# A hybrid decoder layer on one core: attention heads held two and four groups into an ordered stretch, and a longer trail in the output projection's last part

## The chip, the cores and the metric

One core of one Trainium2 chip. The metric is the device time of one launch in microseconds, median of the runs shown; lower is better. Times inside an execution (spans, windows, durations) come from one profiled execution.

## What is computed

One decoder layer on 256 tokens of width 2048, in float32, cut from the reference:

```python
x = layer_norm(alpha * x + 0.5 * swiglu(x, ffn1_w_gate, ffn1_w_up, ffn1_w_down), ln1_g, ln1_b)
p = x @ w_in                                        # columns of both mixers
o_attn = diff_attn_group(p[..., :3072], ...)        # 8 heads, ALiBi, causal, p1 - lam * p2
o_rwkv = rwkv7_group(p[..., 3072:], ...)            # 16 heads of size 64, delta rule over the sequence
mix = concatenate([o_attn, o_rwkv], -1) @ w_out     # (256, 2048) @ (2048, 2048)
x = layer_norm(alpha * x + mix, ln2_g, ln2_b)
x = layer_norm(alpha * x + 0.5 * swiglu(x, ffn2_w_gate, ffn2_w_up, ffn2_w_down), ln3_g, ln3_b)
```

The change lies in the product with `w_out`, in what runs beside it (the last attention heads and the end of the RWKV part), and in its passage to LN2 and the second feed-forward.

## The kernel before

**Products.** All dense products go through one `Stream`. A float32 operand is cut into a high part (`wh`, ScalarE, L142) and the remainder (`wl`, VectorE, L145), and each product becomes three matmuls per 128 rows of K: high by high (L152), high by `wl` (L153), low by high (L154). Activations are cut in the same way by `split` into `xh` (L89) and `xl` (L90). The weights stream in once. A *pair* is two K tiles of 128 rows by 512 columns of weights (512 KB, loaded by SyncE's queue into one of three `raw` buffers). The 256 tokens are two halves, `tt` 0 and 1; a pair is used by each half in turn, six matmuls a half (a *product half*). The loop `block` cuts a pair, runs its first half at once, and puts it on `pend`; the second half runs once more than `lag` pairs are pending. In the stage "mix" there are `nw` = 5 cut buffers, used in turn, and `lag` = 2; the sums of a block of 512 columns go to one of three accumulator banks `acc0` to `acc2`, also in turn, when the block's first product half is issued.

**Background work.** Everything else of the mixers is written as Python generators. After every pair `run_bg` lets them issue a step. Outside the ordered stretch a credit decides how much; in it (`even` is true) each generator issues one step per pair (a step that yields 0 runs on into the next), in the order in which they were started.

**Order on the engines.** Each instruction's engine is fixed by the code; the order of an engine's instructions is made at build time by a planner, which goes by the order of writing as a priority and by its own estimate of when an instruction is ready. All engines then run in order. In two of the output projection's three parts the order on TensorE is not the planner's: `manual_schedule` keeps that part's TensorE instructions in the order of writing. What was written before that stretch is still placed by the planner.

**The output projection.** `W_out` has 16 K tiles: four each of the attention groups 0 and 1 and of the RWKV groups 0 and 1. `parts = [(0, 2), (1,), (3,)]`, so part one multiplies attention group 0 and RWKV group 0 (16 pairs: 4 blocks of 512 columns by 4), part two attention group 1 (8 pairs), part three RWKV group 1 (8 pairs). Before each part `ready` runs to the end the generators that make its operand and cuts the operand by `split`. Parts one and two are the ordered stretch. The pairs of part one are counted here from 0 to 15.

**What runs beside it.** At the start of part one three generators are open. One is the RWKV group 1 chain: it loads its 32 by 32 inverses through ScalarE's DMA queue (`TT<-dY`, L845; `YT`, L849), transposes B and K (L807, copies L809), combines (L858, L869), and runs four chunks (L886, L894, L902, L919, L925). The other two are attention group 1, two heads each: heads 4 and 6, and heads 5 and 7. A head passes these steps, one per pair:

- scores: eight matmuls (L1023) into two banks of tag `at`, read by VectorE (L1025)
- maxima (L1028), exponentials on ScalarE (L1033), scaling and difference (L1035 to L1039)
- transposes (L1044) into a bank `at`, copied to `pT` (L1046; one buffer)
- value product (L1053 to L1055) into a bank `at`, squares of it on ScalarE (L1063, L1066)
- norm: a power on POOL (L1070), VectorE's small steps, and a scaling that reads the bank (L1077)
- transposes back (L1081) into a bank `at`, copied by VectorE into `q` (L1082)

There are two banks `at`. Both generators have passed the transposes of their first head when part one begins, so that both issue the value product after pair 0, the norm after pair 1, and so on; the second heads' scores fall after pair 3.

**The end.** In part three `o_done` adds each finished block to `y` (L326), takes statistics (L328), and after the fourth block `ln_tail` normalises (L341, L349), transposes (L83) and cuts the result as the operand of the second feed-forward. That stage's first block uses seven cut buffers, of which the first five are the same as in the mix stage, beginning again at buffer 0; the last pair of part three holds that buffer. TensorE's order in part three is the planner's.

Of the kernel before, what the change touches and what calls it, by code (L numbers as in the profile page):

```python
# [31 lines left out]
NW = {"ffn": 7, "mix": 5}  # L32
# [7 lines left out]
def build(tc, A, out):  # L40
# [58 lines left out]
    class Stream:  # L99
        def __init__(self):  # L100
            self.pend = []
            self.tail = []
            self.roles = None
            self.behind = []
            self.acc = {}
            self.bg = []
            self.credit = {}
            self.hooks = {}
            self.step = 0
            self.slot = 0  # L110
            self.even = False

        def phase(self, name, pool, banks=None):
            assert not self.pend
            self.name, self.pool, self.banks, self.slot, self.rot = name, pool, banks, 0, 0
            self.buffers(NW[name], LAG[name])
# [170 lines left out]
        def run_bg(self):  # L287
            if self.even:
                for g in list(self.bg):
                    while g in self.bg:  # L290
                        try:
                            if next(g) != 0:
                                break
                        except StopIteration:
                            self.bg.remove(g)
                return
            for g in list(self.bg):
                c = self.credit[g]
                c[0] = min(c[0], 0.0) + c[1]
                while c[0] > 0 and g in self.bg:  # L300
                    try:
                        cost = next(g)
                    except StopIteration:
                        self.bg.remove(g)
                        break
                    if cost is None:
                        break
                    c[0] -= cost
# [13 lines left out]
    stream = Stream()  # L322
# [232 lines left out]
    def mix(mp, pq, C):  # L555
# [87 lines left out]
        def rwkv_start(g, prev=None):  # L643
            gr = Group(g)
            st = {"prev": prev, "group": gr}
            if prev is not None:
                prev["next"] = st
            st["gen"] = rwkv_group(g, st)
            stream.spawn(st["gen"], BG)
            return st  # L650
# [342 lines left out]
        def attn_cols(g):  # L993
            st = {"q": qq[:, g],
                  "k": hp.tile([P, 4, S], F32, tag=HT["k"], name=nm("k"))}

            def qkdone(tt, acc, n):
                chan_major(acc, tt, [P] * 4, lambda tr: SC.copy(out=st[n][:, :, tt * P:(tt + 1) * P], in_=tr))
                if n == "q" and tt == 1:
                    st["left"] = 2  # L1000
                    st["gens"] = [attn_heads(g, st, (i, i + 2)) for i in range(2)]
                    for x in st["gens"]:
                        stream.spawn(x, AT)

            stream.block(w_in, AW + g * NB, NB, KX, x_lhs, lambda tt, acc: qkdone(tt, acc, "k"))
            stream.block(w_in, g * NB, NB, KX, x_lhs, lambda tt, acc: qkdone(tt, acc, "q"))
            return st
# [80 lines left out]
        def gens(*sts):  # L1088
            return [g for st in sts for g in [st.get("gen"), st.get("gen2")] + st.get("gens", []) if g is not None]

        r1 = rwkv_start(0)
        rwkv_cols(0, r1, (1, 0, 2))
        r2 = rwkv_start(1, r1)
        a1 = attn_cols(0)
# [4 lines left out]
        a2 = attn_cols(1)  # L1099
# [7 lines left out]
        def ready(q):  # L1107
            stream.drain(gens((a1, a2, r1, r2)[q]))
            for tt in range(2):
                split(res[q][:, :, tt * P:(tt + 1) * P], oT, tt, q)  # L1110
# [16 lines left out]
        def o_done(tt, acc, n, i):  # L1127
            c = slice(n * NB, (n + 1) * NB)
            if i == 0:
                rc = mp.tile([P, NB], F32, tag="tm", name=nm("rc"), bufs=2)  # L1130
                nc.scalar.dma_start(out=rc, in_=xs[tt][:, c])
                V.scalar_tensor_tensor(out=y[tt][n], in0=rc, scalar=ALPHA, in1=acc, op0=ALU.mult, op1=ALU.add)
            elif i < len(parts) - 1:
                V.tensor_tensor(out=y[tt][n], in0=y[tt][n], in1=acc, op=ALU.add)
            else:
                ln_stats(tt, y[tt][n], acc, st[tt], n)
                if n == 3:
                    ln_tail(tt, y[tt], st[tt], gb[0], gb[1], False)
# [3 lines left out]
        def part(i, qs):  # L1142
            if i == 0:
                yt = [hp.tile([P, 4, NB], F32, tag="J0", name=nm("y")), mp.tile([P, 4, NB], F32, tag="BKc", name=nm("y"))]
                y.extend([yt[n // 2][:, 2 * (n % 2) + t, :] for n in range(4)] for t in range(2))
            if 3 in qs:
                gb.extend(load_gb(mp, A["ln2_g"], A["ln2_b"], "J1", "Q"))
            ks = [(4 * q + j, 4 * q + j) for q in qs for j in range(4)]
            for n in range(4):
                stream.block(A["w_out"][0], n * NB, NB, ks, o_lhs, lambda tt, acc, n=n, i=i: o_done(tt, acc, n, i))  # L1150

        for i, qs in enumerate(parts):
            for q in qs:
                ready(q)
                import os
                if os.environ.get("DBG"): print("DBG", i, q, [(k, x.gi_frame and x.gi_frame.f_lineno) for k, st_ in (("a1",a1),("a2",a2),("r1",r1),("r2",r2)) for x in gens(st_)])
            stream.even = i < len(parts) - 1
            with tc.manual_schedule(engines={mybir.EngineType.PE}) if stream.even else ExitStack():
                part(i, qs)

# [34 lines left out]
    with tc.tile_pool(name="mp", bufs=1) as mp, tc.tile_pool(name="pq", bufs=1, space=bass.MemoryType.PSUM) as pq:  # L1195
        stream.phase("mix", mp)
        mix(mp, pq, C)
        stream.flush()
# [43 lines left out]
```

## Time and profile before

| what | value |
|---|---|
| time, median of 3 runs | 1924.98 us (1924.58 to 1926.66) |
| profiled execution's own time | 1924.33 us |
| its span | 1922.5 us, mean granted TensorE clock 0.992 |
| TensorE busy | 1886.7 us, 98% of the span |
| VectorE, ScalarE, POOL busy | 85%, 57%, 4% |
| HBM traffic | 198 GB/s over the span |
| parts one and two of the output projection | about 1072 to 1183 us |
| part three | about 1183 to 1208 us |

How to read the lines below. A line of the timeline gives start and length in us, engine, line of the kernel, operation, what is written from what, and how many instructions were merged; in brackets stands the idle time of the engine before it and who ended it. A line of waits gives engine, line and releaser, then the total us, the times, and the longest. A line of windows gives the window, its length, and for each engine busy us and instructions, then the granted clock of TensorE (1.00 is full), the share of the DMA engines' time and GB/s. Matmuls overlap, so their rate is read from the distance of their starts. `ACTq` is an instruction that ScalarE's queue spends on a DMA.

### The profile page before, as it was taken

The page shows a single profiled execution, that of the slowest core. Times are in us where ns is not written, and L with a number is a line of the kernel's source. Part 1 is how long each engine was busy: PE and PEld are TensorE (multiplying, and loading weights), DVE is VectorE, ACT ScalarE, POOL GpSimd, SP SyncE. Part 2 cuts the span into 40 slices and gives each one's busy share as a digit, 9 for nine tenths or more (in the row PEclk, how much of TensorE's full clock was granted, in tenths as well). Part 3 has the DMA queues.
Part 4 walks back from the last instruction along what each step waited for, and adds up shares of the span by engine and source line. Part 5 has one row for each costly group of instructions (what it writes and reads, how often), then busy time and mean ns, then how long its engine had stood idle before and what let it go on. Part 6 is the DMA issues. An engine that isn't in the chain of part 4 may idle for free.

```text
span 1922.5 us, 24938 instructions
## 1 busy us (share of the span) xinstructions
PE 1886.7 (98%) x9335; PEld 1551.1 (81%) x9335; DVE 1625.3 (85%) x1834; ACT 1094.3 (57%) x1376; POOL 72.5 (4%) x110
## 2 busy tenths in 40 slices
PE   9999999999999999999999899999999999999997
PEld 7788888888888878887878678788888888888886
DVE  7999987789999976777678767999999778999996
ACT  5656665466666536656555544566666545666651
POOL 0000101100000000000000000000000110000000
PEclk9999999999999999999999899999999999999999
DMA  8756676666667456555445445775566676566744
GB/s 307 250 195 221 186 238 224 223 217 202 218 212 226 139 185 195 169 153 154 143 118 160 135 149 193 245 260 195 192 217 222 210 247 216 197 204 211 232 151 133
DMA packets 207320, 381.72 MB, mean 199 GB/s; under 512 B 23530, under 2 KB 25648, under 8 KB 206944
## 3 DMA queue, kind: packets, MB, share of 16 engines
q1 hardware_dynamic: 182928, 350.53, 55.1%
q0 software_dynamic: 6832, 15.32, 3.0%
q10 hardware_dynamic: 17440, 14.29, 2.5%
q8 instruction: 73, 1.20, 0.2%
q14 instruction: 47, 0.39, 0.1%
HBM read 368.29 MB, written 11.80 MB: 198 GB/s over the span
## 4 chain that ended last, share of the span: by engine, by line
PE 59%; DVE 3%; ACT 1%; issue 1%; DMA 0%; ACTq 0%; DVEq 0%
PE acc L152 18%; PE acc L153 17%; PE acc L154 17%; DVE wl L145 1%; DVE y L341 1%; PE sm L785 1%; DVE y L349 0%; PE tr L580 0%; PE tr L439 0%; PE at L1023 0%; PE pr L727 0%; ACT wh L142 0%; DVE xl L90 0%; PE sm L886 0%; DMA dY<-Y 0%
## 5 line engine op out<-in xcount | busy, mean ns | idle before, releaser
L142 ACT CAST wh<-raw 128x1024 fp32r<-128x1024 f32 (+2 forms) x833 | 852.6, 1047 | 616.2 <-PE acc L154 397.4
L145 DVE TENSOR_TENSOR wl<-raw,wh 128x1024 fp32r<-128x1024 f32 (+2 forms) x833 | 984.0, 1214 | 206.2 <-ACT wh L142 202.0
L153 PE MATMUL acc<-wl,xh 128*128 128x512 f32 (+1 forms) x1552 | 605.7, 392 | 1.1 <-DVE wl L145 1.1
L154 PE MATMUL acc<-wh,xl 128*128 128x512 f32 (+1 forms) x1552 | 604.2, 391 | 0.5 <-DVE xl L90 0.5
L152 PE MATMUL acc<-wh,xh 128*128 128x512 f32 (+1 forms) x1552 | 600.1, 394 | 2.3 <-ACT xh L89 2.3
L152 PEld LDWEIGHTS acc<-wh,xh 128*128 128x128 f32 x1552 | 292.5, 189 | 64.1 <-ACT xh L89 3.8
L154 PEld LDWEIGHTS acc<-wh,xl 128*128 128x128 f32 x1552 | 292.6, 189 | 61.0 <-DVE xl L90 0.9
L153 PEld LDWEIGHTS acc<-wl,xh 128*128 128x128 f32 x1552 | 292.5, 189 | 60.2 <-DVE wl L145 1.7
L223 DVE TENSOR_TENSOR raw<-raw,raw 128x2048 f32<-128x2048 f32 x112 | 256.0, 2286 | 1.6 <-DMA raw<-in_ffn_w_up_dram 0.6
L153 PE MATMUL acc<-wl,hh 128*128 128x512 f32 x544 | 212.0, 390 | 0.0
L154 PE MATMUL acc<-wh,hh 128*128 128x512 f32 x544 | 211.4, 389 | 0.0
L152 PE MATMUL acc<-wh,hh 128*128 128x512 f32 x544 | 210.9, 390 | 0.0
L152 PE MATMUL acc<-wh,s 128*128 128x512 f32 x448 | 175.1, 391 | 1.8 <-ACT acc L249 1.0
L154 PE MATMUL acc<-wh,s 128*128 128x512 f32 x448 | 174.6, 390 | 0.0
L153 PE MATMUL acc<-wl,s 128*128 128x512 f32 x448 | 174.5, 390 | 0.0
L152 PEld LDWEIGHTS acc<-wh,hh 128*128 128x128 f32 x544 | 102.1, 188 | 21.6 <-ACT wh L142 0.4
L153 PEld LDWEIGHTS acc<-wl,hh 128*128 128x128 f32 x544 | 102.1, 188 | 21.1
L154 PEld LDWEIGHTS acc<-wh,hh 128*128 128x128 f32 x544 | 102.1, 188 | 21.0
L152 PEld LDWEIGHTS acc<-wh,s 128*128 128x128 f32 x448 | 84.1, 188 | 20.2 <-ACT acc L249 1.7
L153 PEld LDWEIGHTS acc<-wl,s 128*128 128x128 f32 x448 | 84.1, 188 | 17.8 <-DVE wl L145 0.4
L154 PEld LDWEIGHTS acc<-wh,s 128*128 128x128 f32 x448 | 84.1, 188 | 17.5
L236 ACT COPY acc<-acc 128x512 f32<-128x512 f32 x28 | 16.0, 572 | 51.3 <-PE acc L154 47.5
(264 smaller groups left out, 1099.3 us busy)
## 6 DMA issues: line engine op xcount, KB each, us to landing
raw<-in_ffn_w_up_dram SPq DMA_DIRECT2D x176, 512.0 KB, 5.4
raw<-in_ffn_w_down_dram SPq DMA_DIRECT2D x176, 512.0 KB, 5.3
raw<-in_ffn_w_gate_dram SPq DMA_DIRECT2D x175, 512.0 KB, 4.5
raw<-in_w_in_dram SPq DMA_DIRECT2D x96, 512.0 KB, 3.6
raw<-in_w_out_dram SPq DMA_DIRECT2D x32, 512.0 KB, 3.8
sd<-s POOLq DMA_DIRECT2D x16, 256.0 KB, 4.2
s<-sd POOLq DMA_DIRECT2D x16, 256.0 KB, 4.9
xs<-y ACTq DMA_DIRECT2D x16, 256.0 KB, 3.0
```

The source lines that it names most:

```text
L142: SC.copy(out=wh[:, c, :w], in_=raw[:, c, :w])
L145: self.cut = V.tensor_tensor(out=wl[:, c, :w], in0=raw[:, c, :w], in1=wh[:, c, :w].bitcast(F32), op=ALU.subtract).ins
L152: T.matmul(a, hi, wh[:, j, :w], start=first and j == 0, stop=False, skip_group_check=True)
L153: T.matmul(a, hi, wl[:, j, :w], start=False, stop=False, skip_group_check=True)
L154: i = T.matmul(a, lo, wh[:, j, :w], start=False, stop=last and j == 1, skip_group_check=True)
L223: V.tensor_tensor(out=out, in0=x, in1=y, op=ALU.subtract)
L236: SC.copy(out=u, in_=a)
L341: V.scalar_tensor_tensor(out=y[q], in0=y[q], scalar=mv[:, 0:1], in1=gt[q], op0=ALU.subtract, op1=ALU.mult)
L785: T.matmul(pe[e][:, c, :], BK[r, p, c, e:e + 2].rearrange("p a t -> p (a t)"), AR[r, p, c].rearrange("p a t -> p (a t)"), start=True, stop ...
```

## The change

`Stream` gets a table `hold`. In the ordered stretch `run_bg` passes over a generator as many times as the table says. The two attention generators get 2 and 4: heads 4 and 6 issue their next step after pair 2 instead of pair 0, heads 5 and 7 after pair 4. The RWKV generator is not held. For part three, `buffers(5, 4)` sets `lag` to 4 with the same five cut buffers, so that in the order of writing the second token half trails by four pairs instead of two. A debugging print is dropped.

```diff
@@ class Stream, __init__
             self.even = False
+            self.hold = {}
@@ run_bg
             if self.even:
                 for g in list(self.bg):
+                    if self.hold.get(g):
+                        self.hold[g] -= 1
+                        continue
                     while g in self.bg:
@@ mix, output projection
+        stream.hold = {g: 2 * i + 2 for i, g in enumerate(a2["gens"])}
         for i, qs in enumerate(parts):
             for q in qs:
                 ready(q)
-                import os
-                if os.environ.get("DBG"): print("DBG", ...)
             stream.even = i < len(parts) - 1
+            if not stream.even:
+                stream.buffers(NW["mix"], NW["mix"] - 1)
             with tc.manual_schedule(engines={mybir.EngineType.PE}) if stream.even else ExitStack():
                 part(i, qs)
```

More of the change, by code (lines that the diff above doesn't have):

```diff
@@ L1154, in mix @@
                 ready(q)
-                import os
-                if os.environ.get("DBG"): print("DBG", i, q, [(k, x.gi_frame and x.gi_frame.f_lineno) for k, st_ in (("a1",a1),("a2",a2),("r1",r1),("r2",r2)) for x in gens(st_)])
             stream.even = i < len(parts) - 1
+            if not stream.even:
+                stream.buffers(NW["mix"], NW["mix"] - 1)
             with tc.manual_schedule(engines={mybir.EngineType.PE}) if stream.even else ExitStack():
```

## The prediction

> **What bounds the kernel now.** First the page's busy shares. TensorE is busy 98% of 1922.5 us, so there is no slack elsewhere to harvest: a change that leaves the work as it is can gain only where TensorE waits or runs at a reduced clock.
>
> ```profile
> PE 1886.7 (98%) x9335; PEld 1551.1 (81%) x9335; DVE 1625.3 (85%) x1834; ACT 1094.3 (57%) x1376; POOL 72.5 (4%) x110
> ```
>
> Second, TensorE's waits between 1070 and 1230 us, the stretch that the change touches.
>
> ```profile
> PE at L1044 <- DVE s L1039: 3.2, 1, 3.2
> PE at L83 <- DVE y L349: 3.0, 3, 2.3
> PE at L1053 <- ACT pT L1046: 2.7, 3, 1.4
> PE acc L152 <- ACT xh L89: 1.3, 2, 0.7
> PE at L1023 <- DVE s L1025: 2.5, 1, 2.5
> PE sm L919 <- DVE SV L895: 0.8, 1, 0.8
> ```
>
> Three of the six (8.4 us) are on bank `at`, used here by the attention heads alone; L83 and L152 (4.3 us) are the LN2 junction. Third, the same stretch cut into windows.
>
> ```profile
> core 0: us, PE busy (x) PEld busy (x) DVE busy (x) ACT busy (x) POOL busy (x), PEclk, DMA share, GB/s
> 1073.80:1087.70 13.90, 8.65 (x42) 6.49 (x40) 8.06 (x27) 8.80 (x31) 2.02 (x2) 0.63 0.46 128
> 1087.70:1096.00 8.30, 8.30 (x109) 6.65 (x108) 3.23 (x7) 4.11 (x10) 0.00 (x0) 1.00 0.20 65
> 1096.00:1104.70 8.70, 6.19 (x32) 4.47 (x27) 8.11 (x19) 5.34 (x18) 0.00 (x0) 0.80 0.28 91
> 1208.00:1217.20 9.20, 5.68 (x19) 4.20 (x19) 9.20 (x14) 4.04 (x5) 0.81 (x1) 0.63 0.38 116
> ```
>
> After the column of POOL comes the granted clock: 0.63 and 0.80 in the windows with waits, 1.00 between them. Each wait therefore costs twice, as idle time and as slow matmuls behind it. Fourth, TensorE's timeline, for what the pieces cost fast and slow.
>
> ```profile
> 1073.79 0.49 PE L1044 MATMUL at<-ident,s 128*128 128x128 f32 x3
> 1077.50 0.99 PE L1044 MATMUL at<-ident,s 128*128 128x128 f32 x3 [3.22 <-DVE s L1039]
> 1079.90 0.79 PE L1053 MATMUL at<-v,pT 128*128 128x128 f32 x2 [1.41 <-ACT pT L1046]
> 1083.18 0.63 PE L1055 MATMUL at<-v,pT 128*128 128x128 f32 x2
> ...
> 1090.59 1.02 PE L807 MATMUL sm<-ident,BK 64*128 64x64 f32 x16
> ...
> 1096.01 0.93 PE L1023 MATMUL at<-k,qq 64*128 64x128 f32 x8
> 1099.45 1.38 PE L1023 MATMUL at<-k,qq 64*128 64x128 f32 x8 [2.51 <-DVE s L1025]
> ...
> 1118.20 0.49 PE L1053 MATMUL at<-v,pT 128*128 128x128 f32 x2
> 1118.75 0.39 PE L1055 MATMUL at<-v,pT 128*128 128x128 f32 x2
> 1119.76 0.49 PE L1053 MATMUL at<-v,pT 128*128 128x128 f32 x2 [0.62 <-ACT pT L1046]
> ...
> 1135.56 0.69 PE L886 MATMUL sm<-SV,Q 128*64 128x64 f32 x16
> ...
> 1189.50 0.39 PE L152 MATMUL acc<-wh,xh 128*128 128x512 f32 x1
> ...
> 1190.86 0.39 PE L152 MATMUL acc<-wh,xh 128*128 128x512 f32 x1
> ```
>
> From 1189.50 to 1190.86 lie six matmuls, one product half: 1.36 us at full clock. At full clock a head's value product (L1053 to L1055) takes 0.9 us (1118.20 to 1119.14), three transposes 0.5, sixteen L807 1.0, eight L1023 0.9.
>
> What the waits cost. *Start of the ordered stretch*, 13.9 us: the work in it is two sets of L1044 (1.0), two value products (1.8), one product half (1.4), sixteen L807 (1.0), together 5.2; lost: 8.7. *Fourth pair*, 8.7 us: sixteen L1023 (1.8) and about nine dense matmuls (2.1), 3.9 with rounding; lost: 4.8. *Second heads' value products*: 0.6. In all 14.1 us.
>
> **The change, part by part.** No instruction is added or removed, no DMA either: the moved head stages issue none. The removed debug lines issue nothing.
>
> *1. The first value products move from pair 0 to pairs 2 and 4.* Now TensorE must run both value products before pair 1's half, because the stretch is in written order. They need the second head's transposes, and these need its exponentials:
>
> ```profile
> 1067.36 1.22 DVE L145 TENSOR_TENSOR wl<-raw,wh 128x1024 fp32r<-128x1024 f32 x1
> ...
> 1070.91 0.32 ACTq L845 DMA_DIRECT2D TT<-dY  x1
> ...
> 1074.30 0.40 ACT L1033 ACTIVATE s<-s,mx 128x128 f32<-128x128 f32 x1 [2.41 <-DMA TT<-dY]
> ...
> 1076.54 2.94 ACT L142 CAST wh<-raw 128x1024 fp32r<-128x1024 f32 x3
> ...
> 1077.66 3.50 DVE L145 TENSOR_TENSOR wl<-raw,wh 128x1024 fp32r<-128x1024 f32 x3
> 1087.46 1.20 ACT L809 COPY BT<-sm 128x256 f32<-128x256 f32 x4 [1.79 <-PE sm L807]
> ...
> 1087.75 0.61 DVE L1077 TENSOR_SCALAR ot<-at,ars 128x128 f32<-128x128 f32 x2
> ...
> 1090.69 1.05 ACT L142 CAST wh<-raw 128x1024 fp32r<-128x1024 f32 x1 [2.04 <-PE acc L154]
> ```
>
> ScalarE stands until 1074.30 behind its own queue's TT transfers of the RWKV chain; the change leaves that. The cut at 1090.69 waits for TensorE, as pair 5's must (it takes pair 0's buffer), so the three at 1076.54 are pairs 2 to 4, and pair 1's was done at about 1068.6. After the change TensorE can run pair 1's half (1.4) and the first L807 (1.0) while ScalarE is stuck; with both L1044 sets (1.0) that is 3.4 us of work until pair 2's weights are whole at 1078.8 (1077.66 and a third of 3.50). From 1073.8 that is 5.0 us, so 1.6 remain idle. What is late next is pair 2's cut. The four L809 copies now come ripe before it on ScalarE: 0 to 1.2 more. Slow clock: 0 to 2.4 (after 1099.45 it lasted until 1104.7, some 5 us at half speed). Lost afterwards 1.6 to 5.2; I take 3.1, as the remaining waits are nearest to the short ones. Gain 5.6 (3.5 to 7.1); if the planner still sets the second L1044 ahead of pair 1's half, the 3.2 us wait stays and the gain is about 3.
>
> *2. The second heads' scores move from pair 3 to pairs 5 and 7.* Now both need two `at` banks in one pair and there are two: 2.5 us. Afterwards head 6's scores at pair 5 need the bank of head 5's value product of pair 4, whose release is written behind them (squares on ScalarE, a power on POOL, L1077 on VectorE). That chain ran from 1083.8 (end of L1055) to 1088.4 (end of L1077): 4.6 us. Its cover is pair 5's two halves (2.7) and L886 (0.7): 3.4. Wait 1.2; with one weight cut in its way on each engine (1.05 and 1.2) 3.5. Slow clock again 0 to 2.4. I take 2.3 + 1.2 = 3.5 lost in place of 4.8. Gain 1.3 (from 3.6 down to a loss of 1.1). Behind that wait in TensorE's order stand pair 6's products, and the RWKV chain's next step.
>
> *3. The later value products* fall into pairs 9 and 11; the one `pT` buffer is free by then. Gain 0.6. The heads end at pair 13 instead of 9; part two's first product, pair 16, needs them split (L89, L90). Two pairs of 3.4 us cover that: 0.
>
> *4. The last part trails by four.* TensorE's order is the planner's there.
>
> ```profile
> 1187.71 1.05 ACT L142 CAST wh<-raw 128x1024 fp32r<-128x1024 f32 x1 [3.07 <-PE acc L154]
> 1188.79 1.23 DVE L145 TENSOR_TENSOR wl<-raw,wh 128x1024 fp32r<-128x1024 f32 x1 [1.07 <-ACT wh L142]
> ...
> 1205.34 0.69 DVE L326 TENSOR_TENSOR y<-y,acc 128x512 f32<-128x512 f32 x1 [0.20 <-PE acc L154]
> 1207.64 0.39 PE L154 MATMUL acc<-wh,xl 128*128 128x512 f32 x1
> 1208.04 1.99 ACT L142 CAST wh<-raw 128x1024 fp32r<-128x1024 f32 x2 [1.25 <-PE acc L154]
> 1210.35 1.11 PE L83 MATMUL at<-ident,y 128*128 128x128 f32 x4 [2.33 <-DVE y L349]
> 1212.14 0.80 PE L152 MATMUL acc<-wh,xh 128*128 128x512 f32 x1 [0.68 <-ACT xh L89]
> ```
>
> The first half's last sum is taken at 1205.34 and TensorE stops at 1208.0: two halves trail, where two pairs of written lag leave three. The planner hence already departs from written order. FFN 2 begins at 1212.14, 6.8 us after the sum. More trailing halves would cover that, up to five (6.8 us). But FFN 2's first weights take the buffer of the very last half (cut at 1208.04), so at least 2.3 us (1.05 + 1.23) of the 4.1 us gap stay: gain at most 1.8. Against it: four trailing pairs and the one at work fill all five buffers, so each of pairs 3 to 7 of the part can be cut only when the half four pairs back is through; cut and sum took 2.3 us from 1187.71 to 1190.0, and one half covers 1.4: about 1 us a time. There are three accumulators; the second half's last block now takes the bank of the first half's last block and so waits for L326 (0.7 and hand-over). Covered in part by reordering; I take a loss of 1.0 (bounds: gain 1.8, loss 5 for five bare pairs).
>
> [...] This trace has no wait on wh or wl in the last part; after part 4 five would be the pattern to look for.
>
> **Sum.** 5.6 + 1.3 + 0.6 - 1.0 = 6.5 us off the profiled execution: 1924.33 to 1917.8. The median of the runs shown, 1924.98, is 0.65 above it: 1918.5.
>
> **Rivals.** *(a) More is gained:* the short waits left (1.6 to 2.2, and 2.3) leave the clock at 1.00. Then the slow terms (0.9 and 1.2) go too: 8.6 us, 1916.4, and with the cuts out of the way up to 1912. For it: the 0.62 us wait at 1119.76 was followed by a matmul at its full-speed 0.49. Against it: 2.51 us was enough for 0.80, and 2.33 us at 1210.35 for 0.63. [...]
>
> *(b) The waits only change place:* the second L1044 stays ahead of pair 1 (gain 3) and the bank of part 2 costs its upper bound (loss 1.1): 3 - 1.1 + 0.6 - 1.0 = 1.5, 1923.5. For it: ScalarE's stall is untouched. Against it: pair 1's weights are ready 6 us before its turn, so a planner that looks for ready work finds it.
>
> *(c) Slower:* in the last part TensorE runs in written order, and every one of the five cuts is waited for bare: 2.4 us each, 12 us, with the clock down up to as much again. That outweighs the 7.5 us of parts 1 to 3 from the fourth bare cut on: 1924.98 - 7.5 + 12 = 1929.5 or more. Against it: the planner's departure shown above.
>
> **How the numbers follow.** The measurement tells 0.2%, 3.85 us, from no change: the borders are 1921.1 and 1928.8. My case 0.50 (1916.5 to 1921), (a) 0.20, (b) 0.21, (c) 0.09. Faster is mine and (a), 0.70; no change is (b), 0.21; slower is (c), 0.09. The range reaches through (b) and most of (a), to 1913 and 1925.5; (c) and the tail of (a) are left out.
>
> **What will show it.** Right: no L1044 wait of 3 us, a product half and L807 ahead of the second L1044; the clock above 0.63 between 1074 and 1088; L1023 in two separate pairs, the first with a wait of 1 to 3.5 us whose releaser is L1077 or L1025. Part 4: three or four trailing halves after the first half's last sum, waits on wh or wl of about 1 us in the last part, and FFN 2's first product still 6.8 us or more after that sum. Wrong: a new wait of part two on L89 for the late heads, or TensorE waiting between pairs on the RWKV chain, whose steps now have less head work between them.

## The result, and the profile after

The changed kernel takes 1921.53 us (median of 12 runs, 1917.74 to 1925.42); the kernel before 1925.37 (12 runs, 1924.49 to 1927.47). The ratio is 0.9978, 95% interval 0.9969 to 0.9987: 3.8 us faster, just past the 0.2% that can be told from no change. Forecast were 1918.5 and a range of 1913 to 1925.5.

The profiled execution is one of the slower ones (1923.39 us, span 1921.6), so the profile is read by stretches. First, TensorE's waits between 1060 and 1235 us:

```profile
PE acc L154 <- DVE wl L146: 4.0, 3, 2.7
PE at L1027 <- DVE ot L1081: 2.4, 1, 2.4
PE acc L153 <- DVE y L330: 1.5, 1, 1.5
PE at L1048 <- DVE s L1043: 1.0, 1, 1.0
PE acc L153 <- ACT wh L143: 0.9, 1, 0.9
PE at L83 <- DVE y L353: 0.6, 1, 0.6
PE sm L83 <- DVE y L353: 0.5, 1, 0.5
```

The line numbers of the changed kernel are 1 larger up to `run_bg` and 4 larger behind it: L1027 is the scores' matmul, L1048 the head transposes, L1081 the norm's scaling, L146 the cut `wl`, L330 the sum into `y`. The waits of 3.2 and 2.5 us at the heads' transposes and scores are now 1.0 and 2.4, those on `pT` are gone, and the last part has three kinds that it had not: on `wl`, on `wh`, and on `y` (an accumulator that is not read yet).

Second, windows of the changed kernel (the columns are those of the prediction's windows; the clock is the one after POOL):

```profile
1073.80:1084.60 10.80, 9.18 (x45) 6.75 (x43) 4.92 (x9) 6.64 (x17) 0.00 (x0) 0.84 0.44 102
...
1098.40:1108.50 10.10, 7.69 (x37) 5.46 (x36) 6.56 (x21) 3.16 (x12) 1.01 (x1) 0.66 0.31 95
...
1178.00:1203.00 25.00, 22.85 (x98) 17.63 (x96) 17.55 (x22) 7.37 (x7) 0.00 (x0) 1.00 0.50 156
1203.00:1208.30 5.30, 4.32 (x13) 3.45 (x14) 5.20 (x10) 1.90 (x2) 1.01 (x1) 0.68 0.49 157
1208.30:1222.00 13.70, 9.97 (x38) 7.48 (x37) 13.70 (x22) 4.40 (x7) 1.00 (x1) 0.75 0.67 237
```

The start of the ordered stretch went from 0.63 of the clock (over 13.9 us) to 0.84 (over 10.8); the scores of the second head (1098.40 to 1108.50) still cost a slow stretch; and the last part, 1178 to 1208, where TensorE was busy without a break before, now has idle time and, at its end, a clock of 0.68.

Third, what lies between three fixed points of the program: the last scores ahead of the ordered stretch (L1023, now L1027), the last RWKV value (L975, now L979) at the end of it, and a product of the second feed-forward (L439, now L443). The rows of one line's instructions in a window (count, durations, first and last start) of the kernel before:

```profile
L1023 PE MATMUL at<-k,qq x14: 272/376/480, 1060.8 to 1068.1; 64*128 64x256 f32 x8, 64*128 64x128 f32 x6
L975 PE MATMUL sm<-gs,g x8: 379/379/379, 1169.8 to 1175.0; 128*128 128x256 f32 x8
```

of the changed kernel:

```profile
L1027 PE MATMUL at<-k,qq x14: 272/376/480, 1061.7 to 1069.0; 64*128 64x256 f32 x8, 64*128 64x128 f32 x6
L979 PE MATMUL sm<-gs,g x8: 379/379/379, 1164.4 to 1169.6; 128*128 128x256 f32 x8
```

and the third point in TensorE's timeline, before:

```profile
1403.09 1.03 PE L439 MATMUL tr<-ident,sg 128*128 128x128 f32 x8
```

and after:

```profile
1401.65 1.03 PE L443 MATMUL tr<-ident,sg 128*128 128x128 f32 x8
```

Ordered stretch (first to second point): 1175.0 - 1068.1 = 106.9 us before, 1169.6 - 1069.0 = 100.6 after, 6.3 less. Last part and passage (second to third): 1403.09 - 1175.0 = 228.1 before, 1401.65 - 1169.6 = 232.05 after, 4.0 more. In this profile the change is two changes of opposite sign. These lengths are given below for the kernels on which the argument rests.

The last part's new waits, in TensorE's timeline of the changed kernel, and what VectorE did ahead of the longest but one:

```profile
1191.77 0.50 PE L153 MATMUL acc<-wh,xh 128*128 128x512 f32 x1 [0.85 <-ACT wh L143]
...
1201.05 0.50 PE L154 MATMUL acc<-wl,xh 128*128 128x512 f32 x1 [0.76 <-DVE wl L146]
...
1203.98 0.79 PE L153 MATMUL acc<-wh,xh 128*128 128x512 f32 x1 [1.51 <-DVE y L330]
...
1207.99 0.39 PE L155 MATMUL acc<-wh,xl 128*128 128x512 f32 x1
...
1214.50 0.79 PE L154 MATMUL acc<-wl,xh 128*128 128x512 f32 x1 [2.69 <-DVE wl L146]
```

```profile
1200.91 0.68 DVE L330 TENSOR_TENSOR y<-y,acc 128x512 f32<-128x512 f32 x1
1201.51 1.22 DVE L146 TENSOR_TENSOR wl<-raw,wh 128x1024 fp32r<-128x1024 f32 x1
1202.64 0.69 DVE L332 BATCH_NORM_STATS2 st<-y 128x6 f32<-128x512 f32 x1
1203.25 0.67 DVE L330 TENSOR_TENSOR y<-y,acc 128x512 f32<-128x512 f32 x1
```

At 1203.98 the last block of the second half waits for the accumulator of the first half's last block. VectorE reads it at 1203.25, behind a cut of 1.22 and the statistics. The matmul after it takes 0.79 in place of 0.39: the clock has fallen.

### The profile page after: what moved, and what is told of

The parts are those of the page before. It is cut to its first block, busy times and chain, and to the rows that moved or that the text cites. A ratio compares the mean times of both kernels' runs of the same rounds, so it can differ in the third digit from the quotient of the medians.

```text
span 1921.6 us, 24939 instructions
## 1 busy us (share of the span) xinstructions
PE 1888.3 (98%) x9335; PEld 1551.5 (81%) x9335; DVE 1625.3 (85%) x1834; ACT 1094.9 (57%) x1376; POOL 73.7 (4%) x110
## 5 line engine op out<-in xcount | busy, mean ns | idle before, releaser
L146 DVE TENSOR_TENSOR wl<-raw,wh 128x1024 fp32r<-128x1024 f32 (+2 forms) x833 | 984.3, 1216 | 206.8 <-ACT wh L143 202.7
L154 PE MATMUL acc<-wl,xh 128*128 128x512 f32 (+1 forms) x1552 | 607.3, 393 | 5.2 <-DVE wl L146 5.2
L154 PEld LDWEIGHTS acc<-wl,xh 128*128 128x128 f32 x1552 | 293.7, 189 | 65.6 <-DVE wl L146 6.8
L154 PE MATMUL acc<-wl,hh 128*128 128x512 f32 x544 | 212.0, 390 | 0.0
L154 PE MATMUL acc<-wl,s 128*128 128x512 f32 x448 | 174.3, 389 | 0.0
L154 PEld LDWEIGHTS acc<-wl,hh 128*128 128x128 f32 x544 | 102.1, 188 | 21.0
L154 PEld LDWEIGHTS acc<-wl,s 128*128 128x128 f32 x448 | 84.1, 188 | 17.3
```

Of the source, the lines that this page charges most:

```text
L146: self.cut = V.tensor_tensor(out=wl[:, c, :w], in0=raw[:, c, :w], in1=wh[:, c, :w].bitcast(F32), op=ALU.subtract).ins
L154: T.matmul(a, hi, wl[:, j, :w], start=False, stop=False, skip_group_check=True)
```

## The experiments

In all of them "hold" is the table `hold` with `run_bg`'s three lines, "trail" the `buffers` line of the last part.

**1. Hold alone.** The change without this:

```diff
-            if not stream.even:
-                stream.buffers(NW["mix"], NW["mix"] - 1)
```

> The change without its last edit: heads held two and four pairs, the last part trails by two as before. Theory H (the two edits have opposite signs): in the changed kernel's profile the ordered stretch is 6.2 us shorter and the last part with the passage to FFN 2 3.9 us longer, so the hold alone gives 1919 (before 1925.4, the full change 1921.5), and the last part shows no wait on wh, wl or y. Theory N (the longer trail is about free, as the prediction's 1.0, and the profiled execution's loss there is chance of the clock): the hold alone gives 1920.5 to 1921.5.

Measured 1915.94 (1913.67 to 1918.16) against 1925.31: 9.4 us faster, ratio 0.9951 (0.9938 to 0.9963). That is 3.1 below the 1919 of theory H, whose gain had the right sign and was too small. Ordered stretch 96.3 us, last part and passage 228.4. The second length is that of the kernel before (within 0.3), so the trail alone made the 4.0 us. The first is 4.3 shorter than the full change's, although TensorE's order in that stretch is the same; experiment 9 and the last section come back to this.

**2. Trail alone.** The two lines that experiment 1 leaves out are added to the kernel before; the table `hold` stays empty.

> The last edit alone: heads as before, the last part trails by four. Theory H: 3.9 us slower than before, 1929.3 (between 2.5 and 5.5 slower), with waits on wh or wl of about 0.8 us each and one of 1.5 us on y (the accumulator bank) in the last part. Theory N: within 1 us of before.

Measured 1928.57 (11 runs, 1927.41 to 1931.5), ratio 1.0017 (1.0009 to 1.0026): 3.3 us slower, as theory H says. The profiled execution is its slowest, 1931.5. Its point two, by the rows of that line, and its point three, by the timeline:

```profile
L979 PE MATMUL sm<-gs,g x8: 379/379/379, 1173.8 to 1179.0; 128*128 128x256 f32 x8
```

```profile
1410.27 1.03 PE L443 MATMUL tr<-ident,sg 128*128 128x128 f32 x8
```

231.3 us, 3.2 more than before; the last part's waits are the same (`y` 1.5, `wh` 0.9, `wl` 0.8). From the last L979 to the last product of `w_out` it takes 38.5 us, in the full change 38.4, before 32.6: in the last part the trail costs the same with or without the heads. The passage behind it differs.

**3. Hold two and three.** The heads one pair apart, no trail: `2 * i + 2` becomes `i + 2`.

> Hold of two and three pairs, trail of two. Head 5's value product then lies a pair earlier and its bank is released by steps written ahead of head 6's scores. Theory B (the 2.4 us wait at head 6's scores is the chain from value product to L1081 on that bank, 4.6 us against 3.4 us of cover): the wait and the slow clock behind it (window at 0.66) go, and a new wait under 1 us stands at head 5's transposes back, which need the bank of head 6's scores; 3 to 5 us faster than the hold of two and four alone, 1914 to 1916. Rival S (the wait is VectorE's or ScalarE's load at that place, not the bank): it stays at 2 us or more and the time is that of the hold of two and four.

Measured 1919.47 (1916.39 to 1921.73) against 1925.31, ratio 0.9967 (0.9955 to 0.9979). Theory B's 1914 to 1916 did not come. Rival S has the wait right but not the time, which is 3.5 us above experiment 1 by the medians (the intervals overlap at their edges). The wait at the second head's scores is 2.14 us, hardly less than the 2.41 of four pairs, though the bank's chain begins 5.5 us earlier. VectorE's timeline says why:

```profile
1093.00 0.41 DVE L1068 TENSOR_SCALAR ot<-at 128x256 f32<-128x256 f32 x1
...
1094.09 1.23 DVE L146 TENSOR_TENSOR wl<-raw,wh 128x1024 fp32r<-128x1024 f32 x1 [0.53 <-ACT wh L143]
1095.24 0.67 DVE L874 COPY TT<-sm 32x512 f32<-32x512 f32 x1
...
1097.04 0.16 DVE L1072 TENSOR_SCALAR vr<-ss 128x2 f32<-128x2 f32 x1
...
1098.42 1.21 DVE L146 TENSOR_TENSOR wl<-raw,wh 128x1024 fp32r<-128x1024 f32 x1
1099.55 0.15 DVE L1079 TENSOR_TENSOR ars<-ars 128x2 f32<-128x2 f32 x1
1099.73 0.61 DVE L1081 TENSOR_SCALAR ot<-at,ars 128x128 f32<-128x128 f32 x2
```

The norm's small steps (L1068 to L1081, most of them 0.16 us) stand in VectorE's order behind two cuts and copies of other steps. From the product's end at 1090.2 to L1081's end at 1100.3 the chain takes 10.1 us, 7.3 of them from L1068 on. In the full change it is 6.1 (1095.7 to 1101.9), 4.2 from L1068 on, with one cut between. What set the bank free was VectorE's place for L1081 far more than the head start of the product; this is read from two traces, and no run moves L1081 alone.

**4. A fourth accumulator bank for the last part**, with hold and trail:

```diff
+                stream.nacc = 4
...
-                self.rot = (i + 1) % NACC[self.name]
+                self.rot = (i + 1) % (self.nacc or NACC[self.name])
+            if i == 3 and self.name == "mix":
+                return self.banks.tile([P, NB], F32, tag="pr", name=nm("acc"), bufs=1)
```

> The full change with a fourth accumulator bank in the last part (the bank of tag pr, free by then). Theory A (the three accumulators in turn cost: the second half's first block cannot start before the first half's second block is summed, and the last block's second half waits for the last sum): the 1.5 us wait on y goes, and with it the slow clock there; 2 to 4 us faster than the full change, 1917.5 to 1919.5. Rival C (the five cut buffers alone cost): the waits on wh and wl stay or grow, and the time is that of the full change, 1921.5 within 1.

Measured 1919.06 (1918.52 to 1920.55) against 1925.31, ratio 0.9967 (0.9954 to 0.9979): 6.2 us faster, 2.4 more than the full change, theory A. The 1.5 us wait on `y` is gone. Two waits on `wl` are on record (line numbers are 3 larger than the full change's: L157 is L154), and between them the last product of `w_out`:

```profile
1081.71 0.50 PE L157 MATMUL acc<-wl,xh 128*128 128x512 f32 x1 [0.59 <-DVE wl L149]
...
1202.09 0.39 PE L158 MATMUL acc<-wh,xl 128*128 128x512 f32 x1
...
1208.18 0.79 PE L157 MATMUL acc<-wl,xh 128*128 128x512 f32 x1 [1.07 <-DVE wl L149]
```

The first is pair 2's cut at the start of the ordered stretch, which experiment 1 has too; the second lies in the passage. In the last part TensorE waits for nothing: from the last L982 (at 1169.4) to the last product it takes 32.7 us, as before the change (32.6). So with the five cut buffers unchanged, the bank alone ends the waits on `wh` and `wl` there as well. Last part and passage: 227.9 us, 4.1 less than the full change in the two profiles; the medians say 2.4. By the medians the kernel is still 3.1 above experiment 1 on the same chip (the intervals overlap); the two profiles are 2.6 apart, of which 2.2 lie in the ordered stretch (98.5 and 96.3) and none in the last part.

**5. Hold two and two.** Both generators after pair 2, no trail: `2 * i + 2` becomes `2`.

> No four-pair trail; both heads of a group are held for two pairs, so their value products stand together behind pair 2 and their next scores together at pair 5. This does part 1 of the change (start of the ordered stretch) without the separation of part 2. Theory A (the two parts add up, each wait with its slow clock): the start gains what was foreseen, 5.6 us, and the eight score products of pair 5 keep the wait of 2.5 us of the kernel before: 1919.7 (1918 to 1921.5). Theory B (without the waits of the start the clock no longer falls at the scores; the wait costs only itself): 1917.3. Theory C (the separation is worth nothing, since separated scores also wait 2.4 us): the same as both heads held two and four pairs without the trail, 1916 (1914.5 to 1917).

Measured 1920.02 (1917.99 to 1924.32) against 1926.49, ratio 0.9968 (0.9957 to 0.9979): 6.5 us faster, theory A. One detail differs: the eight scores wait 1.4 and the two value products 2.6 us in two, where the expectation had only the 2.5 at the scores. Part 1 is worth 6.5, and the separation (parts 2 and 3) the rest of experiment 1, about 2.9. The two intervals overlap at their edges, so the 2.9 is not firm.

**6. Hold two and five**, no trail: `3 * i + 2`.

> No four-pair trail; the heads of a group are held for two and five pairs, so that the second head's scores fall to pair 8 in place of 7. Theory A (the 2.41 us wait at the second head's scores is the first head's norm chain, 6 us, outlasting its cover; a further pair covers it): no wait of over 1 us at the score products, 2.4 us less than with two and four pairs: 1913.5 (1912.5 to 1915). Rival B (VectorE's queue only hands the wait to the next user of the bank, a value product or the third heads' transposes): the wait turns up at another line of the heads and the time stays at 1916 (1915 to 1917.5).

Measured 1915.52 (1915.12 to 1918.19) against 1926.49, ratio 0.9945 (0.9932 to 0.9957). Rival B: the 2.4 us wait is gone, and the value product written behind the scores now waits 1.4 us for a bank:

```profile
PE at L1057 <- DVE s L1029: 1.4, 1, 1.4
```

Against two and four pairs no difference can be told.

**7. TT and YT from GpSimd's queue**, hold, no trail; the two `nc.scalar.dma_start` at L849 and L853 become `nc.gpsimd.dma_start`.

> No four-pair trail, heads held two and four pairs, and the RWKV chain's TT and YT transfers are issued from GpSimd's queue in place of ScalarE's. Theory A (ScalarE stands behind its own queue's transfers until 1074.3, which holds the exponentials and so the second head's transposes): the wait of 1.0 to 1.2 us at the transposes goes, and so does what it costs in clock: 1914.5 (1912.5 to 1915.5). Rival B (the transfers themselves end the wait wherever they are issued: the RWKV chain's first step needs TT as well): the wait moves to the RWKV chain's first products, the time stays at 1916 (1915 to 1918).

Measured 1927.27 (1925.74 to 1928.71), ratio 1.0001 (0.9992 to 1.001): the whole gain is gone, and neither theory foresaw it. The exponentials went at 1073.58 in place of 1077.02 (experiment 1) and the wait at the transposes vanished, as A says. But the RWKV chain's first product waits for YT:

```profile
PE sm L862 <- DMA YT<-dYT: 7.6, 1, 7.6
```

The writes `dY` and `dYT`, from which TT and YT are read back, go from ScalarE at 1081.61 and 1082.19 in place of 1068.17 and 1069.35. That is late mostly because what they write is late. The last step that makes `Y` on VectorE, in experiment 1 and then here:

```profile
1067.96 0.18 DVE L836 TENSOR_TENSOR Y<-Y,itmp 64x31 f32<-64x31 f32 x1
```

```profile
1079.83 0.18 DVE L836 TENSOR_TENSOR Y<-Y,itmp 64x31 f32<-64x31 f32 x1
```

With TT's reads on another queue the planner set these steps of VectorE 11.9 us later, and `dY` follows 1.6 us behind.

**8. The fourth bank without the trail** (hold and the bank).

> No four-pair trail, heads held two and four pairs, and the fourth accumulator bank in the output projection's last part, with the trail of two pairs. It asks whether the bank is worth 2.5 us by itself or only to the trail of four. Theory A (the bank only takes away the wait that the trail of four makes): 1916 (1914.5 to 1917.5), no difference to the same kernel with three banks. Rival B (the bank frees the planner's order in the last part whatever the trail): 1913.5 (1912 to 1914.5).

Measured 1918.54 (1914.56 to 1918.81) against 1926.49, ratio 0.9950 (0.9936 to 0.9964): by the ratio the same as hold alone, by the medians 8.0 us faster where hold alone was 9.4. The median lies 1 us above theory A's range, and further from rival B's. No worth of the bank by itself can be seen.

**9. Hold alone again**, on the chip of the next two.

> The kernel with both heads held two and four pairs and no four-pair trail once more, on the chip of the next two, as their measure. Expected 9.4 us below the kernel before (8 to 11).

Measured 1915.33 (1914.33 to 1919.09) against 1925.93, 10.6 us faster, ratio 0.9949 (0.9936 to 0.9961). Its profiled execution is its slowest run, 1919.09; that of experiment 1, on another chip, took 1915.94. The program is the same, so the two profiles show what differs between runs. The second head's scores in TensorE's timeline, then the window around them; first of experiment 1:

```profile
1101.44 0.92 PE L1027 MATMUL at<-k,qq 64*128 64x128 f32 x6 [2.41 <-DVE ot L1081]
```

```profile
1090.00:1110.00 20.00, 17.59 (x203) 13.73 (x196) 16.20 (x41) 10.06 (x24) 2.01 (x2) 1.00 0.38 121
```

and of this run:

```profile
1102.02 1.64 PE L1027 MATMUL at<-k,qq 64*128 64x128 f32 x6 [2.41 <-DVE ot L1081]
```

```profile
1090.00:1110.00 20.00, 17.59 (x198) 13.59 (x191) 14.91 (x40) 9.35 (x24) 2.02 (x2) 0.83 0.37 114
```

The wait is 2.41 us in both. In one the clock stays at 1.00, in the other it is 0.83 over 20 us: 3.4 us of full-speed work lost. The ordered stretch is 96.3 in the one and 99.9 in the other, 3.6 apart. At its start the two differ also: this run waits 0.2 us at the transposes where experiment 1 waits 1.2, but has a further 3.41 us at half rate (1.7 lost; the granted clock from 1073.8 to 1090 reads 0.89), which nearly cancels.

**10. Fourth bank and a sixth pair of weight buffers**, with hold and trail. The sixth buffer lies in tiles that nothing else uses by then:

```diff
-                stream.buffers(NW["mix"], NW["mix"] - 1)
+                stream.buffers(NW["mix"] + 1, NW["mix"] - 1)
...
+            if i == 5 and self.name == "mix":
+                wh, wl = (hp.tile([P, 2, NB], F32R, tag=HT[x], name=nm(t)) for t, x in (("wh", "k"), ("wl", "lw")))
```

> The whole change with the fourth accumulator bank and a sixth pair of weight buffers in the output projection's last part (in tiles that nothing else uses by then). Theory A (the trail of four costs 2.5 us by the bank and the other 2 to 3 us by the cuts, which find no free buffer): no wait on wh or wl of over 1 us before the last product of w_out, and the time of the kernel without the trail: no more than 1.5 us above or below it. Rival B (what the trail costs beside the bank is the passage to FFN 2, whose first weights wait for the last trailing half): still 2 to 4 us more than without the trail, the time going behind the last product of w_out.

Measured 1915.99 (1914.2 to 1916.91) against 1925.93, ratio 0.9945 (0.9932 to 0.9959): the time of hold alone on the same chip (1915.33). Its point two by the rows of that line, its point three by the timeline, and its largest wait (its line numbers are 6 larger than the full change's: L985 is L979):

```profile
L985 PE MATMUL sm<-gs,g x8: 379/379/379, 1163.7 to 1168.9; 128*128 128x256 f32 x8
```

```profile
1395.70 1.03 PE L449 MATMUL tr<-ident,sg 128*128 128x128 f32 x8
```

```profile
PE at L83 <- DVE y L359: 2.9, 3, 2.4
```

226.8 us for last part and passage, 5.2 less than the full change and 1.3 less than before; the 1.3 goes with the clock, at half rate for 3.41 us in the passage where the kernel before has 6.83 (from 1203 to 1226 it reads 0.93 here, 0.85 before). No product of the last part waits for a cut or an accumulator, and it takes 32.7 us, as in experiment 4. Theory A's time came true, but its split is not borne out: experiment 4 left no loss in the last part for the sixth buffer to take away. By the medians the buffer adds 3.7 to experiment 4, but the intervals of the two overlap. The longest wait at the passage (L83) is back at 2.4 us, as large as before the change.

**11. dY and dYT from GpSimd's queue too**, otherwise as 7.

> Heads held two and four pairs, no four-pair trail; the RWKV chain's transfers TT and YT and also the writes dY and dYT ahead of them are issued from GpSimd's queue, so that the order of ScalarE no longer sets when they go. Theory A (in the run with TT and YT alone moved, the planner set dY's issue 15 us later on ScalarE, and that made the 7.6 us wait): the wait on YT is gone or below 1 us, the wait at the transposes too, and the time is 0 to 2 us below the kernel with the heads held alone. Rival B (GpSimd's issues are late in themselves, 0.7 us for each of eight): a wait on YT of 2 us or more stays, 2 to 6 us above it.

Measured 1926.21 (1924.89 to 1928.81), ratio 1.0001 (0.9992 to 1.001). A wait on YT of 7.2 us stays, and the time is 10.9 us above experiment 9; rival B's sign, at twice its size. GpSimd's queue:

```profile
1075.44 0.59 POOL L840 DMA_DIRECT2D dY<-Y  x1 [11.15 <-DVE Y L836]
1079.97 2.16 POOL L849 DMA_DIRECT2D TT<-dY  x3 [3.94 <-DMA dY<-Y]
1085.93 0.66 POOL L849 DMA_DIRECT2D TT<-dY  x1 [3.80 <-issue]
1086.58 0.52 POOL L841 DMA_DIRECT2D dYT<-U  x1
1091.39 1.29 POOL L853 DMA_DIRECT2D YT<-dYT  x2 [4.30 <-DMA dYT<-U]
```

The issues themselves take 0.5 to 0.7 each, so rival B's reason is not it. Two other things are late. `Y` is, as in experiment 7:

```profile
1074.95 0.18 DVE L836 TENSOR_TENSOR Y<-Y,itmp 64x31 f32<-64x31 f32 x1
```

That is 7.0 us later than in experiment 1, nearly the whole wait. And `dYT` is set behind all reads of `dY`, so that the queue stands twice for a write to land, 3.94 and 4.30 us. Which of the two would have been enough by itself is open; no run parts them. ScalarE's stall (2.41 us before, 3.23 in experiment 1) was a smaller price than either kernel's wait on YT.

## Why the prediction was right or wrong

The time, 1921.53, lies 3.0 above the predicted one, and the sign was right. That it lies so near is in part luck: by the medians the heads gained 1.9 more than foreseen and the trail lost 4.5 more, and the two errors work against each other. By its own steps:

| step | foreseen | shown |
|---|---|---|
| 1 to 3, the heads | gain 7.5 | 9.4 and 10.6 by the medians of experiments 1 and 9 |
| 1, start of the stretch | gain 5.6 (3.5 to 7.1) | 6.5 (experiment 5) |
| 2 and 3, scores apart | gain 1.9 | about 2.9 (experiments 1 and 5) |
| 4, the trail | loss 1.0 (up to 5) | 3.2 and 4.0 by profiles; 3.3 alone and 5.5 on top of the heads by medians (9.4 less 3.8) |

*Part 1* was right in its working. The idle time left, foreseen as 1.6 on pair 2's cut, is 1.0 at the transposes and then 0.6 on that cut, the same in sum:

```profile
1079.08 0.30 PE L1048 MATMUL at<-ident,s 128*128 128x128 f32 x1 [1.03 <-DVE s L1043]
...
1080.53 0.68 PE L154 MATMUL acc<-wl,xh 128*128 128x512 f32 x1 [0.58 <-DVE wl L146]
```

The planner did set pair 1's half and L811 ahead of the second transposes. By windows laid over the ordered stretch, TensorE's idle time in it fell from 9.4 us to 4.2 in the full change and 4.3 in experiment 1. The rest of the gain is the clock, at half rate for 13.65 us there before and for 0 to 10.24 after; that differs from run to run.

*Part 2* put the wait at 2.3 us and it is 2.41, with L1081 as releaser. But 2.3 was a value between bounds. The chain was taken as 4.6 us with a cover of 3.4; it took 6.1 with a cover of 3.8. A weight cut in VectorE's order, counted in the upper bound only, stood in the chain here (one cut) and in experiment 3 (two). The slow clock was put at a fixed 1.2: it is 0 (experiment 1), 1.7 (experiment 8) or 3.4 (experiment 9); from 1090 to 1110 the clock reads 1.00, 0.91 and 0.83.

*Part 3* was right: no wait at the value products is left.

*Part 4* is the term that was mis-sized. The prediction named two mechanisms, buffers and accumulator, priced the accumulator at 0.7 us and a hand-over, and then took 1.0 in all because the planner departs from written order. It does, but with three accumulators it has too little to depart with: the waits of 0.85, 0.76 and 1.51 us remained (3.1 together) and the last drew a slow clock at 0.68 over 5.3 us, 1.7 more. These 4.8 are most of what the last part grew by: from the last L979 to its last product at 1207.99 it took 38.4 us, from the last L975 to 1207.64 before 32.6, 5.8 more. 1.8 came back at the passage, as the bound had it: from the last product to the marker of FFN 2 it is 193.7 us, before 195.5. Net 4.0. The accumulator is what costs: with a fourth one and the same five buffers the last part takes 32.7 us, without any wait (experiment 4). "Three or four trailing halves" was wrong: two trail, as before. FFN 2's first product came 7.0 us after the first half's last sum (6.8 foreseen at the least), and then its `wl` was 2.69 late. The new waits on `wh` and `wl` look like too few cut buffers, but the buffer that was short is not the one that the waits name: with a fourth accumulator alone they are gone, and so is the last part's loss.

*Rival (a)*, that short waits leave the clock alone, holds in some runs of the kernel and not in others; hold alone comes to its 1916.4, by chance, as that figure has the loss of part 4 in it. *Rival (b)* had the time nearly right, in the main for a wrong reason. Its first mechanism did not occur. The price of its second was reached in the profiled execution, by the clock rather than the wait (2.41 and 3.4 lost, against 3.5 and 2.4), but not in experiment 1 (2.41 alone). The loss that did occur, in the last part, is not in it. *Rival (c)*, five bare cuts, did not occur: two cuts showed, at 0.85 and 0.76.

Settled: the heads' move gains, the trail takes back 3.3 to 5.5 of the 9.4, and in the last part the accumulator bank is the whole of its price. Open: whether the sixth buffer is worth anything. The medians, each kernel against its own runs of before, give 2.4 to the bank and 3.7 to the buffer; the profiles give 4.1 and 1.1, and the 1.1 goes with a slow stretch that is 3.41 us shorter. Open also: why the trail costs more by the medians on top of the heads (5.5) than alone (3.3). The intervals are wide, and the profiles put the difference between the full change and experiment 1 that is not in the last part and passage into the ordered stretch, where the clock differs. The fastest kernels, hold alone (two and four, or two and five pairs) and the one of experiment 10, cannot be told apart at 1915 to 1916. Of these, hold alone is the smallest edit.

## What to carry to other kernels

A longer trail is paid in resources: count the cut buffers and the accumulators that must be live at once. Here one accumulator short lengthened the last part by 5.8 us. The tile that a wait names need not be the one that is short: the waits on `wh` and `wl` went when an accumulator was added. When a wait is for a bank, look at where its reader stands in its engine's order, not at when the bank's data was ready. And two edits of opposite sign in one change hide each other: fixed points of the program, with their distance in both traces, part them. Where a run-to-run difference of the clock lies in the same stretch, even these lengths need a second profile (the ordered stretch of one program took 96.3 us in one and 99.9 in another).

## What the runs showed of the hardware

Around this change (1070 to 1230 us) the half-rate clock came in stretches of 3.41 us and multiples of it: 10.24, 3.41 and 6.83 us in the trace of the kernel before; 3.41 and 6.83, twice each, in that of the changed kernel. A window laid on one of them reads 0.50, so each 3.41 costs 1.7 us of work. Whether a given wait draws one is not a matter of its length alone: the same 2.41 us wait left the clock at 1.00 in one execution and took it to 0.83 over 20 us in another of the same program. Six profiles with the same order of TensorE in the ordered stretch (the full change, experiments 1, 4, 8, 9, 10) took 100.6, 96.3, 98.5, 100.8, 99.9 and 101.3 us for it, a spread of 5.0, about three times 1.7. Half rate took 10.24 us of it in the full change. By the clocks from 1073.8 to 1090 and from 1090 to 1110 it took as much in experiment 8 (0.79 and 0.91) and in 9 and 10 (0.89 and 0.83 in both). In experiment 1 the clock from 1090 to 1110 reads 1.00, and between the stretch's start and 1108 no dense matmul takes more than 0.50 us. For experiment 4 it is not shown. The full change's runs spread by 7.7 us and go with their mean clock: 0.995 in the five fastest (1917.74 to 1920.77), 0.992 or 0.993 in the five slowest (1923.39 to 1925.42).

The traces of the kernel before and of the changed kernel show one thing more. Half rate begins at 1077.07, 1100.96 and 1210.19 before, that is 7 and 32 times 3.41 us apart, and at 1080.69, 1101.17, 1203.57 and 1213.81 after, 6, 30 and 3 times apart; the ends of these stretches lie on the same grid. By windows laid on single steps of it, TensorE stood idle for 2.79, 1.90 and 2.17 us before, and for 1.62, 1.67, 1.87 and 2.47 us after, in the full-rate step just ahead of each stretch. In eleven other full-rate steps of the two traces between 700 and 1230 us it stood idle for 0.74 to 1.51 us, and the clock stayed at 1.00 in the step behind. In the others the idle time is less, and none of them has half rate behind it. The idle time of one wait can fall into one step or be shared by two, which fits the two outcomes of the 2.41 us wait. But no row of experiments 1 and 9 gives the place of their grid, and no run sets it on purpose: that it parts the two is not shown.
